# Weight tiles of the projections at multiples of 512 bytes in each partition, in a two-layer hybrid trunk

## The chip, the cores and the metric

The kernel runs on one core of a Trainium2 chip. The metric is the device time of one execution in microseconds; the kernel before is given by the median of three runs. A profiled execution of the same kernel gives the rows that are read here. Engines are named as in the profile: PE is TensorE's matmul, PEld its loading of the stationary operand, DVE is VectorE, ACT ScalarE, POOL GpSimd, SP the engine that issues the weight transfers.

## The reference

Two layers work on 256 tokens of width 2048, in float32. A layer normalises its input, multiplies it by one wide matrix, runs four token mixers of width 512 on the parts (forgetting attention, differential attention, a state-space recurrence in chunks, a diagonal state-space scan), and merges them with gates:

```python
xn = _rmsnorm(h, pre_norm_g[l])
(fq, fk, fv, ff, fg, dq, dk, dv, dg, sz, sxbc, sdt, su, sg, mg) = _combined_projection(xn, w_in[l])
oa = _forgetting_attention(...) * jax.nn.silu(fg)
ob = _differential_attention(...) * jax.nn.silu(dg)
oc = _ssd_branch(sz, sxbc, sdt, ...)
od = _s5_branch(su, ...) * jax.nn.silu(sg)
merged = None
for n, o in enumerate((oa, ob, oc, od)):
    gate = jax.nn.sigmoid(mg[..., n * D_MODEL:(n + 1) * D_MODEL])
    term = gate * (o.astype(h.dtype) @ w_branch[l, n])
    merged = term if merged is None else merged + term
y = merged @ w_out[l]
h = h + _rmsnorm(y, post_norm_g[l])
```

By far the most arithmetic is in the projections: `xn @ w_in`, `o @ w_branch`, the small matrix of the last mixer, and `merged @ w_out`, each with 256 tokens on one side.

## The kernel before, in words

A projection is cut into groups of 512 output columns (one group, `bc`, has 524). `plan()` lists the groups of a layer in the order in which they run. `group()` computes one of them for two blocks of 128 tokens. For each k-tile (128 rows of the weights) it issues three matmuls for token block 0 and three for block 1, all of 512 columns. The factor three comes from the number format: each weight w and each activation x is split into a high and a low part in float32r, and the product is taken as xh·wh + xh·wl + xl·wh (L387, L388, L389). In these matmuls the activation part is the stationary operand and the weight tile is streamed. In the rows `acc<-wh,xh` the streamed tile is named first.

The weights come in chunks of four k-tiles (1 MB) on SP's queue into `raw`, which has three buffers. `prefetch()` then makes two pairs of tiles of each chunk, each for two k-tiles: ScalarE copies `raw` into `wh` (L104), VectorE subtracts to get `wl` (L92). The pools whp and wlp have five buffers each, and take turns. So ten k-tiles go once round the five buffers. Buffers of a pool are all as big as the largest tile in it, 2 x 524 floats, that is 4192 bytes in each partition.

The first chunk, and some chunks around the last projection of each layer, take another way: with `spread=True` the four k-tiles are split one by one into tiles of the pool `blkp` (names bwh and bwl), which has 37 buffers of 2048 bytes in each partition and holds most other activations of a layer too. In the last group of each layer and the first of layer 1 the second token block comes 16 k-tiles behind the first (`lag`). In the program as built, where the framework orders instructions anew by what is ready, the two blocks of layer 1's first group alternate on different k-tiles at the end; in the last group of layer 1 block 0 runs through all k-tiles before block 1. In all other groups the two blocks take each k-tile in turn, so that block 1 reads the weight tile that block 0 has just read.

The stationary tiles (xh, xl, mh, ml from the pool actp; oh, ol, gh, gl from blkp) start at multiples of 512 bytes.

The mixers run between the projections. After each chunk `pump()` takes pieces of them from a queue, up to a budget of VectorE time, and issues them on all engines. Their small matmuls and transposes stand in TensorE's own order between two chunks of a projection. Transposes and several masks use the table `cs`, which is in the first pool, cp, with the residual stream `h` and the parameters.

Pools lie one after the other in each partition in the order in which they are opened: cp, rawp, whp, wlp, actp, blkp, tp. In the kernel as built, `cs` starts at byte 32,896, the first raw buffer at 40,448, the first wh at 65,600, the first wl at 86,560, the first stationary tile of actp at 107,520 and the first blk at 140,288.

Of the kernel before, what the change touches and what calls it, by code (L numbers as in the profile page):

```python
# [10 lines left out]
F32 = mybir.dt.float32  # L11
F32R = mybir.dt.float32r
# [6 lines left out]
L, D, T = 2, 2048, 256  # L19
NBLK = 37  # L20
NW = 5
AHEAD = 1
BUDGET = 1.7
# [3 lines left out]
W = 512  # L27
# [3 lines left out]

# w_in column offsets of the segments
SEG = dict(fq=0, fk=512, fv=1024, ff=1536, fg=1540, dq=2052, dk=2564, dv=3076, dg=3588,
           sz=4100, xs=4612, B=5124, C=5380, dt=5636, su=5644, sg=6156, mg=6668)

# columns of the constant table
C_ID, C_U, C_ST, C_MK, C_COS, C_SIN, C_ONE, NCST = 0, 128, 256, 384, 640, 704, 832, 833
# columns of the per-partition parameter table
P_PRE, P_CW, P_CB, P_ARE, P_AIM, P_LDT, P_D, NPRM = 0, 16, 48, 56, 72, 88, 104, 108
# columns of the row (broadcast) parameter table  # L40
R_B12, R_ALOG, R_SD, R_SUB, NROW = 0, 12, 20, 28, 156


def plan():
    """Order in which one layer consumes its weights: (kind, argument, columns per k-tile, k-tiles)."""
    p = []
    for s in ("fq", "fk", "fv", "bc", "fg", "dq", "dk", "dv", "dg", "xs", "sz", "su", "sg"):
        p.append(("in", s, 524 if s == "bc" else 512, KT))
    for n in range(3):
        for cg in range(4):  # L50
            p.append(("mg", (n, cg), 512, KT))
            p.append(("br", (n, cg), 512, 4))
    for cg in range(4):
        if cg == 3:
            p.append(("glu", 0, 512, 4))
            p.append(("glu", 1, 512, 4))
        p.append(("mg", (3, cg), 512, KT))
    for cg in range(4):
        p.append(("br", (3, cg), 512, 4))
    for cg in range(4):  # L60
        p.append(("out", cg, 512, KT))
    return p
# [3 lines left out]
def trunk(ctx: ExitStack, tc: tile.TileContext, x, xT0, wall, cst, prm, rows, lam, normg, postg, s5b, s5c, out):  # L66
# [3 lines left out]

    cp = ep(tc.tile_pool(name="cp", bufs=1))
    rawp = ep(tc.tile_pool(name="rawp", bufs=3))
    whp = ep(tc.tile_pool(name="whp", bufs=NW))
    wlp = ep(tc.tile_pool(name="wlp", bufs=NW))
    actp = ep(tc.tile_pool(name="actp", bufs=2))
    blkp = ep(tc.tile_pool(name="blkp", bufs=NBLK))
# [12 lines left out]

# [1 line left out]
    def tt(out, a, b, op):  # L91
# [17 lines left out]
    order = [None]  # L109

    def load(out_, in_):
        """on the queue of the weights, in the order of the calls."""
        if order[0] is None:
            order[0] = nc.sync.dma_start(out=out_, in_=in_).ins
        else:
            with tc.issue_after(order[0]):
                order[0] = nc.sync.dma_start(out=out_, in_=in_).ins

# [1 line left out]
    h = [cp.tile([128, D], F32, name=f"h{tb}") for tb in range(2)]  # L120
# [14 lines left out]
    one = cs[:, C_ONE:C_ONE + 1]  # L135

# [1 line left out]
    def rsqrt(dst, ss, n, inv, eps):  # L138
        """dst = 1/sqrt(ss*inv + eps), all [128, n]."""
        v, y, t, p = (small([128, n], f"rq_{c}{n}") for c in "vytp")  # L140
        ts(v, ss, inv, eps, MUL, ADD)
        ts(y.bitcast(I32), v.bitcast(I32), -0.5, 1597463007.0, MUL, ADD)
        for i in range(2):
            if n == 1:
                stt(t, y, v, y, MUL, MUL)
            else:
                tt(t, y, y, MUL)
                tt(t, t, v, MUL)
            ts(p, t, 0.375, -1.25, MUL, ADD)
            tt(t, t, p, MUL)  # L150
            last = V.scalar_tensor_tensor(out=dst if i else y, in0=t, scalar=1.875, in1=y, op0=ADD, op1=MUL)
        return last.ins
# [35 lines left out]

# [1 line left out]
    ex1 = cp.tile([128, L, 26], F32, name="ex1")  # L190
# [6 lines left out]
    def params():  # L197
# [20 lines left out]
        dt = ex1[:, :, 10:26]  # L218
# [3 lines left out]
        yield 1.3  # L222
        # theta and 16*theta, reduced to [-pi, pi], then sin and cos of a quarter, doubled twice
        sh = [128, 2, L, 16]
# [30 lines left out]
        yield 0.5  # L255
        # k = (exp(lam dt) - 1) / lam
        kr, ki_ = S5K[:, 0], S5K[:, 1]
# [20 lines left out]

# [1 line left out]
    def split_T(dst, src, nt, scale=None, gcol=None):  # L280
        """src [128, nt*128] -> dst(i) = (hi, lo), each [128, 128], of the scaled transpose of block i;
        dst(None) = both for all blocks at once."""
        ps = mx()
# [16 lines left out]

# [1 line left out]
    chunks = [ncol for _ in range(L) for _, _, ncol, nk in plan() for _ in range(nk // 4)]  # L302
# [3 lines left out]
    behind = [None]  # L306

    def prefetch(spread=False):
        """loads the next chunk of four k-tiles and splits it into its two float32r parts."""
        ncol = chunks[woff[1]]  # L310
# [14 lines left out]
        for hf in range(2):  # L325
            wh = whp.tile([128, 2, ncol], F32R, tag="wh", name="wh")
            wl = wlp.tile([128, 2, ncol], F32R, tag="wl", name="wl")
            act(wh, raw[:, 2 * hf:2 * hf + 2])
            split_lo(wl, raw[:, 2 * hf:2 * hf + 2], wh)
            loaded.extend((wh[:, kk], wl[:, kk]) for kk in range(2))  # L330
# [8 lines left out]
    queue = []  # L339
# [28 lines left out]
    def group(stat, nk, ncol, evac, budget=BUDGET, lag=0, hook=None):  # L368
        """acc[tb] = stat(tb)^T @ W for one group of columns, token block 1 some k-tiles behind block 0;
        evac(tb, acc) takes each block's."""  # L370
        cuts = [(0, 512)] if ncol == 512 else [(0, ncol // 2), (ncol // 2, ncol // 2)]
# [29 lines left out]

# [1 line left out]
    def pipeline(n, stages, step):  # L403
        """item i's stage j runs in step i + j*step; each stage gives its cost on VectorE."""
        for t in range(n + (len(stages) - 1) * step):
            cost = 0.0
            for j, f in reversed(list(enumerate(stages))):
                if 0 <= t - j * step < n:
                    cost += f(t - j * step)
            yield cost  # L410

    def headpair_T(dst, src, hp, scale=None):
        """dst [128, 2 heads, 256 tokens] from the token-major src[tb]."""
        ps = mx().rearrange("p (h t) -> p h t", h=2)
# [6 lines left out]
    def probs_T(E, nb):  # L421
        """transposes of E [128 q, nb*128] -> [128 k, nb, 128 q] in SBUF."""
        ps = mx()
# [11 lines left out]
    def fox(st):  # L435
# [8 lines left out]
        for kb in range(2):  # L444
# [7 lines left out]
            p3 = ps.rearrange("p (h k) -> p h k", h=4)  # L452
            # lf is -log_sigmoid, so its running sum enters with a plus
            for hd in range(4):
# [141 lines left out]
    def ssd(st):  # L596
# [9 lines left out]
        yield WAIT  # L606
        # decay from each token to the end of chunk 0, and from the start of chunk 1 to each token
        psd = mx()
# [3 lines left out]
        act(dec, psd[:, 0:16], AF.Exp)  # L612
        # the running sums' addends in two exact float32r parts
        Ah, Al = small([128, 2, 8], "Ah", F32R), small([128, 2, 8], "Al", F32R)
# [66 lines left out]
        for tb in range(2):  # L681
# [6 lines left out]
            for g in range(2):  # L688
                L3 = LT[2 * tb + g].rearrange("p (h t) -> p h t", h=4)
                tt(L3, L3, Gm[tb][:, g:g + 1].to_broadcast([128, 4, 128]), MUL)  # L690
                yield 0.6
        # state after chunk 0, and its way into chunk 1
        pst = mx()
# [38 lines left out]
    def s5(st):  # L732
        l = st["l"]
        # tables exp(i theta t), t = 0..15 and 16*(0..15); re/im: which, tile, power
        E1 = [blk("E1", (128, 2, 16, 16)) for _ in range(2)]
# [7 lines left out]
        while n < 16:  # L743
            # power n = (power n/2)^2, then powers n+1 .. 2n-1
            hr, hi = E1[0][:, :, :, n // 2], E1[1][:, :, :, n // 2]
# [19 lines left out]
            n *= 2  # L765
        # C' = C * k
        cr = [blk("s5c", (128, 16, 32)) for _ in range(2)]
# [142 lines left out]

# [1 line left out]
    def new_act(name):  # L912
# [11 lines left out]
    for l in range(L):  # L924
        ss = small([128, 2, 4], "hss")
        st = dict(l=l)
        # transposed input times the gain, not normalised; 1/rms goes in where the products leave PSUM
        if l == 0:
# [98 lines left out]
        for gi, (kind, arg, ncol, nk) in enumerate(plan()):  # L1027
# [70 lines left out]
            else:  # L1098
# [8 lines left out]
                def residual(tb, last):  # L1107
                    """h += y / rms(y) * gain; then the next layer's input, or the output."""
                    s1, r1 = small([128, 1], "ys1"), small([128, 1], "yr1")
# [29 lines left out]

# [1 line left out]
def _layout(i):  # L1141
# [88 lines left out]
```

## Time and profile before

| | |
|---|---|
| median of 3 runs | 1813.01 us (1811.5 to 1814.68) |
| span of the profiled execution | 1811.1 us |
| TensorE busy | 1793.2 us, 8348 matmuls |
| VectorE busy | 1318.5 us |
| ScalarE busy | 862.1 us |
| DMA | 331.32 MB, mean 183 GB/s |

The span runs from the first to the last instruction. In the rows, a matmul is given with the time at which it starts and the time until its result is through, and neighbouring matmuls overlap in that; the pace of TensorE is therefore read from the distances between starts. The granted clock (PEclk) is a share of full speed: 1.00 is the upper of its two levels, 2.4 GHz.

### The profile page before, as it was taken

How to read it: one execution, taken by the hardware profiler on the slowest of the kernel's cores; microseconds unless marked ns; L12 is line 12 of the kernel's file. 1: busy time of each engine (PE TensorE's matmuls, PEld its weight loads, DVE VectorE, ACT ScalarE, POOL GpSimd, SP SyncE). 2: the span in 40 equal slices, each digit the busy share in tenths (PEclk: the TensorE clock that was granted, in tenths of full speed). 3: DMA queues.
4: the chain of work that ended last, by engine and by line, in shares of the span. 5: the costliest groups of instructions: out<-in, count | busy, mean ns of one | idle time of the engine just before them, and what ended most of it. 6: DMA issues, size and time to landing. Idle time of an engine off the chain costs nothing.

```text
span 1811.1 us, 21982 instructions
## 1 busy us (share of the span) xinstructions
PE 1793.2 (99%) x8348; PEld 1460.4 (81%) x8348; DVE 1318.5 (73%) x2358; ACT 862.1 (48%) x1171; POOL 16.5 (1%) x34
## 2 busy tenths in 40 slices
PE   8999999999999999999999999999999999999997
PEld 6888877888878787788879888788888787877886
DVE  6764478887798879765674645689777988787744
ACT  6445445545444444444464454555444444444442
POOL 0000000000000000000000000000000000000000
PEclk9999999999999999999999999999999999999999
DMA  9554543455555545555545445434554554556552
GB/s 344 191 185 149 193 172 134 174 186 197 186 194 180 184 163 210 193 188 179 186 184 188 163 163 186 163 140 172 203 178 162 198 209 175 178 197 208 183 187 94
DMA packets 49434, 331.32 MB, mean 183 GB/s; under 512 B 6064, under 2 KB 6192, under 8 KB 10800
## 3 DMA queue, kind: packets, MB, share of 16 engines
q1 hardware_dynamic: 46928, 322.05, 50.1%
q0 software_dynamic: 2400, 7.87, 1.2%
q8 instruction: 65, 1.06, 0.2%
q14 instruction: 41, 0.34, 0.1%
HBM read 327.80 MB, written 2.10 MB: 182 GB/s over the span
## 4 chain that ended last, share of the span: by engine, by line
PE 97%; DMA 1%; DVE 1%; ACT 0%; issue 0%; SPq 0%; DVEq 0%; ACTq 0%
PE acc L388 30%; PE acc L387 30%; PE acc L389 30%; PE mx L285 1%; DMA raw<-in_wall_dram 1%; PE mx L549 1%; PE mx L433 1%; PE mx L418 1%; PE mx L877 0%; PE mx L846 0%; PE mx L815 0%; PE mx L706 0%; PE mx L425 0%; PE mx L467 0%; DVE wl L92 0%; DVE h L101 0%
## 5 line engine op out<-in xcount | busy, mean ns | idle before, releaser
L92 DVE TENSOR_TENSOR wl<-raw,wh 128x1024 fp32r<-128x1024 f32 (+1 forms) x586 | 714.2, 1223 | 397.6 <-ACT wh L104 396.6
L104 ACT ACTIVATE wh<-raw 128x1024 fp32r<-128x1024 f32 (+1 forms) x586 | 620.4, 1060 | 788.9 <-PE acc L389 731.2
L387 PE MATMUL acc<-wh,xh 128*128 128x512 f32 (+1 forms) x1896 | 737.1, 389 | 0.0
L388 PE MATMUL acc<-wl,xh 128*128 128x512 f32 (+1 forms) x1896 | 735.1, 388 | 0.5 <-DVE wl L92 0.5
L389 PE MATMUL acc<-wh,xl 128*128 128x512 f32 (+1 forms) x1896 | 733.2, 387 | 0.0
L387 PEld LDWEIGHTS acc<-wh,xh 128*128 128x128 f32 x1896 | 356.3, 188 | 78.7 <-issue 3.8
L388 PEld LDWEIGHTS acc<-wl,xh 128*128 128x128 f32 x1896 | 356.4, 188 | 76.9 <-issue 2.0
L389 PEld LDWEIGHTS acc<-wh,xl 128*128 128x128 f32 x1896 | 356.4, 188 | 76.7 <-issue 0.7
L387 PE MATMUL acc<-wh,oh 128*128 128x512 f32 x256 | 101.4, 396 | 0.0
L389 PE MATMUL acc<-wh,ol 128*128 128x512 f32 x256 | 100.8, 394 | 0.0
L388 PE MATMUL acc<-wl,oh 128*128 128x512 f32 x256 | 100.8, 394 | 0.0
L387 PE MATMUL acc<-wh,mh 128*128 128x512 f32 x224 | 88.6, 396 | 0.0
L388 PE MATMUL acc<-wl,mh 128*128 128x512 f32 x224 | 88.4, 394 | 0.0
L389 PE MATMUL acc<-wh,ml 128*128 128x512 f32 x224 | 88.3, 394 | 0.0
L104 ACT ACTIVATE sig<-acc,rhalf 128x512 f32<-128x512 f32 x64 | 44.0, 688 | 32.1 <-PE acc L389 28.6
L389 PEld LDWEIGHTS acc<-wh,ol 128*128 128x128 f32 x256 | 48.1, 188 | 11.1
L388 PEld LDWEIGHTS acc<-wl,oh 128*128 128x128 f32 x256 | 48.1, 188 | 10.7
L387 PEld LDWEIGHTS acc<-wh,oh 128*128 128x128 f32 x256 | 48.1, 188 | 10.6
L389 PEld LDWEIGHTS acc<-wh,ml 128*128 128x128 f32 x224 | 42.1, 188 | 9.7
L387 PEld LDWEIGHTS acc<-wh,mh 128*128 128x128 f32 x224 | 42.1, 188 | 9.6
L388 PEld LDWEIGHTS acc<-wl,mh 128*128 128x128 f32 x224 | 42.1, 188 | 9.5
L864 DVE TENSOR_TENSOR_SCAN s5a<-S5R,s5w 128x256 f32<-128x256 f32 x64 | 40.9, 676 | 0.0
(331 smaller groups left out, 1336.4 us busy)
## 6 DMA issues: line engine op xcount, KB each, us to landing
raw<-in_wall_dram SPq DMA_DIRECT2D x291, 1024.0 KB, 4.8
raw<-in_wall_dram SPq DMA_DIRECT2D x8, 1048.0 KB, 4.9
s5b<-in_s5b_dram POOLq DMA_DIRECT2D x16, 256.0 KB, 3.7
xr<-in_xT_dram SPq DMA_DIRECT2D x8, 256.0 KB, 9.1
h<-in_x_dram SPq DMA_DIRECT2D x2, 1024.0 KB, 8.8
pg<-in_postg_dram POOLq DMA_DIRECT2D x8, 256.0 KB, 4.3
out_dram<-h SPq DMA_DIRECT2D x8, 256.0 KB, 2.8
s5c<-in_s5c_dram POOLq DMA_DIRECT2D x4, 256.0 KB, 4.6
```

Source lines behind the costliest of these rows:

```text
L92: V.tensor_tensor(out=out, in0=a, in1=b, op=op)
L104: A.activation(out, a, f, **kw)
L285: PE.transpose(ps[:, i * 128:(i + 1) * 128], src[:, i * 128:(i + 1) * 128], ident)
L387: PE.matmul(o, lhsT=sh, rhs=rh, start=k == 0, stop=False)
L388: PE.matmul(o, lhsT=sh, rhs=rl, start=False, stop=False)
L389: PE.matmul(o, lhsT=sl, rhs=rh, start=False, stop=k == nk - 1)
L418: PE.transpose(ps[:, i, tb * 128:(tb + 1) * 128], src[tb][:, c:c + 128], ident)
L433: PE.matmul(pso[:, c], lhsT=pt[:, b], rhs=v[b][:, c], start=b == 0, stop=b == nb - 1)
L549: PE.matmul(ps[:, a, 0:nk], lhsT=qT[hd // 2][64 * a:64 * a + 64, hd % 2, qb * 128:(qb + 1) * 128], rhs=kT[hd // 2][64 * a:64 * a + 64, hd ...
L864: V.tensor_tensor_scan(out=a[:, r], data0=rr, data1=w[:, r], initial=0.0, op0=MUL, op1=ADD)
```

## The change

Each tile of wh and wl now begins at a multiple of 512 bytes in its partition. Three edits do it: a tile `pad` of 112 floats (448 bytes) is the first of the pool cp and moves everything behind it; the tiles of the 524-column group are allocated 576 columns wide and used only in their first 524, so that a buffer has 4608 bytes; and a tile `pad2` of 384 floats (1536 bytes) stands in the pool wlp. Nothing is written to the pads or read from them. Instructions, their order and their sizes are otherwise the same. The places of the tiles behind the weights move by 6144 bytes in all. The diff, without comments that it also drops:

```diff
 NBLK = 37
 NW = 5
+KW = 576
+PAD = 112
...
     cp = ep(tc.tile_pool(name="cp", bufs=1))
+
+    pad = cp.tile([128, PAD], F32, name="pad")
     rawp = ep(tc.tile_pool(name="rawp", bufs=3))
     whp = ep(tc.tile_pool(name="whp", bufs=NW))
     wlp = ep(tc.tile_pool(name="wlp", bufs=NW))
+
+    pad2 = wlp.tile([128, 384], F32, tag="pad2", name="pad2", bufs=1)
     actp = ep(tc.tile_pool(name="actp", bufs=2))
...
         for hf in range(2):
-            wh = whp.tile([128, 2, ncol], F32R, tag="wh", name="wh")
-            wl = wlp.tile([128, 2, ncol], F32R, tag="wl", name="wl")
+            kw = ncol if ncol == 512 else KW
+            wh = whp.tile([128, 2, kw], F32R, tag="wh", name="wh")[:, :, 0:ncol]
+            wl = wlp.tile([128, 2, kw], F32R, tag="wl", name="wl")[:, :, 0:ncol]
             act(wh, raw[:, 2 * hf:2 * hf + 2])
```

## Rows read from the trace of the kernel before

**Rows 1.** The page: busy us and share by engine; the chain that ended last.

```profile
PE 1793.2 (99%) x8348; PEld 1460.4 (81%) x8348; DVE 1318.5 (73%) x2358; ACT 862.1 (48%) x1171; POOL 16.5 (1%) x34
...
PE 97%; DMA 1%; DVE 1%; ACT 0%; issue 0%; SPq 0%; DVEq 0%; ACTq 0%
```

**Rows 2.** TensorE's longest wait: us in all, times, longest us.

```profile
PE acc L387 <- ACT bwh L104: 6.9, 2, 6.6
```

**Rows 3.** TensorE's groups by form: count, busy us, mean ns of one.

```profile
L387 PE MATMUL acc<-wh,xh 128*128 128x512 f32 x1768 | 700.6, 396 | 0.0
...
L387 PE MATMUL acc<-wh,oh 128*128 128x512 f32 x256 | 101.4, 396 | 0.0
...
L387 PE MATMUL acc<-wh,mh 128*128 128x512 f32 x224 | 88.6, 396 | 0.0
...
L387 PE MATMUL acc<-wh,xh 128*128 128x262 f32 x128 | 36.4, 285 | 0.0
...
L387 PE MATMUL acc<-wh,gh 128*128 128x512 f32 x32 | 12.8, 399 | 0.0
...
L425 PE MATMUL mx<-cs,E 128*128 128x128 f32 x48 | 10.8, 279 | 0.2 <-ACT pt L104 0.2
...
L285 PE MATMUL mx<-cs,m 128*128 128x128 f32 x64 | 8.3, 272 | 0.0
```

**Rows 4.** Timeline, last projection of layer 1: starts of some k-tiles (block 0).

```profile
1731.51 0.39 PE L387 MATMUL acc<-wh,mh 128*128 128x512 f32 x1
...
1735.67 0.39 PE L387 MATMUL acc<-wh,mh 128*128 128x512 f32 x1
...
1737.05 0.39 PE L387 MATMUL acc<-wh,mh 128*128 128x512 f32 x1
...
1739.83 0.39 PE L387 MATMUL acc<-wh,mh 128*128 128x512 f32 x1
...
1741.24 0.39 PE L387 MATMUL acc<-wh,mh 128*128 128x512 f32 x1
...
1745.41 0.39 PE L387 MATMUL acc<-wh,mh 128*128 128x512 f32 x1
...
1753.73 0.39 PE L387 MATMUL acc<-wh,mh 128*128 128x512 f32 x1
...
1755.14 0.39 PE L387 MATMUL acc<-wh,mh 128*128 128x512 f32 x1
```

**Rows 5.** Timeline, last group of layer 1, tiles from blk, 23 steps.

```profile
1784.31 0.39 PE L387 MATMUL acc<-bwh,mh 128*128 128x512 f32 x1
...
1785.47 0.39 PE L389 MATMUL acc<-bwh,ml 128*128 128x512 f32 x1
...
1789.55 0.39 PE L389 MATMUL acc<-bwh,ml 128*128 128x512 f32 x1
```

**Rows 6.** Timeline, first group of layer 1, tiles from blk, 27 steps.

```profile
923.68 0.39 PE L387 MATMUL acc<-bwh,xh 128*128 128x512 f32 x1
...
929.80 0.39 PE L389 MATMUL acc<-bwh,xl 128*128 128x512 f32 x1
```

**Rows 7.** Stages: us, busy PE, PEld, DVE, ACT, POOL, clock, DMA share, GB/s.

```profile
923.40:930.00 6.60, 6.60 (x30) 5.45 (x30) 5.86 (x15) 4.13 (x7) 0.00 (x0) 1.00 0.95 371
...
500.00:550.00 50.00, 50.00 (x231) 39.99 (x230) 45.61 (x74) 23.38 (x28) 1.08 (x2) 1.00 0.50 179
```

**Rows 8.** Timeline: first and last of 133 cuts in the projections.

```profile
60.54 1.03 PE L418 MATMUL mx<-cs,fq 128*128 128x128 f32 x8
...
1716.73 1.04 PE L285 MATMUL mx<-cs,m 128*128 128x128 f32 x8
```

**Rows 9.** Splits on VectorE: count, ns least/median/most, first and last start.

```profile
L92 DVE TENSOR_TENSOR wl<-raw,wh x586: 1194/1225/1253, 15.2 to 1777.3; 128x1024 fp32r<-128x1024 f32 x191, 128x1048 fp32r<-128x1048 f32 x5
```

**Rows 10.** Timeline, first group of layer 0, last steps of its first chunk.

```profile
14.30 0.39 PE L389 MATMUL acc<-bwh,xl 128*128 128x512 f32 x1
...
14.98 0.39 PE L389 MATMUL acc<-bwh,xl 128*128 128x512 f32 x1
```

## The prediction

> **What bounds the kernel now.** I read the page first. TensorE is busy 1793.2 of the 1811.1 us of the span, and the chain that ended last is TensorE for 97% [rows 1]. The waits say that nothing starves it: its longest kind of wait on another engine adds up to 6.9 us in two places [rows 2]. So weights are ready early, and the time is the number of matmuls times the distance from one start to the next. Busy time hides that distance, because matmuls overlap (each row shows some 395 ns, while a new one starts every 230 ns). I therefore went to the timeline of TensorE and subtracted starts.
>
> Almost all of the work is 512 columns wide and reads a weight tile from the pools of wh and wl: by the groups kept apart by form, L387 has 1768 + 256 + 224 + 32 = 2280 of them, and L388 and L389 as many each, 6840 in all [rows 3]. In the last projection of layer 1 a k-tile is six such matmuls in a row (L387, L388, L389 for token block 0, then for block 1). Ten k-tiles use each of the five buffers of the pool once, with both halves of it. One such round, 60 matmuls, runs from 1731.51 to 1745.41: 13.90 us, or **231.67 ns a matmul**. The reader should see that the k-tiles within it are unequal and that the inequality comes back: the one that starts at 1735.67 takes 1.38 us, the one at 1739.83 takes 1.41 us, and a round later, at 1753.73, the same place in the round takes 1.41 us again [rows 4]. Same shape, same engine state, other buffer: what differs is where in a partition the tile lies. The code gives the places. A buffer of wh or wl holds 2 x 524 floats, 4192 bytes, which is 8 x 512 + 96; so the five buffers start at five different remainders of 512 (64, 160, 256, 352, 448 for wh, 32, 128, 224, 320, 416 for wl, adding up the tiles in front of them).
>
> The trace of before also holds the other case. For the first chunk, and around the last projection of each layer, `prefetch(spread=True)` puts weight tiles into the blk pool (bwh, bwl), whose buffers of 2048 bytes start at multiples of 512 (the first at 140,288 = 274 x 512). They go through the same three lines with the same activations. From 1785.47 to 1789.55 there are 18 steps in 4.08 us: **226.67 ns a matmul** [rows 5]. And with both token blocks interleaved, 27 steps from 923.68 to 929.80 take 6.12 us: again 226.67 [rows 6]. That is not a quiet moment: in the window around the second stretch VectorE is busy 5.86 of 6.60 us, ScalarE 4.13, the DMA engines 95%, and the granted clock is 1.00, as elsewhere [rows 7]. So neither neighbours nor clock explain the 5 ns.
>
> **The change, part by part.** *The weight tiles.* The pad ahead of everything adds 448 bytes, which brings the first wh buffer from 65,600 to 66,048 = 129 x 512; 576 columns instead of 524 make a buffer 4608 bytes = 9 x 512; the second pad (1536 bytes) keeps wl at a multiple of 512 and makes the total shift of the later pools 448 + 10 x 416 + 1536 = 6144 = 12 x 512, so activations and the blk pool keep their remainders. All 6840 matmuls then read from places like those of bwh and bwl. Gain if each goes from 231.67 to 226.67 ns: 6840 x 5.00 ns = **34.2 us**. All of it is on the path, since TensorE is the path.
>
> *What is not gained.* The pace has to settle: when bwh tiles follow wh tiles at 1784.31, the first 5 steps take 1.16 us to 1785.47, where 5 x 226.67 would be 1.133 us, so 0.027 us too much [rows 5]. I charge this once after each interruption. Other matmuls cut the stream of projections 133 times (counted along the timeline, the first and the last in [rows 8]): 133 x 0.027 = 3.6 us. The last step before and the first after a cut have lengths of their own (the first after the cut of [rows 8] lies in the wake of other work), so I take no gain on 2 x 133 steps: 266 x 5 ns = 1.3 us. Net: 34.2 - 3.6 - 1.3 = **29.3 us**.
>
> *The 262-column matmuls* (group bc; 128 on each line at 285 ns [rows 3]) start at multiples of 512 only in part: the second k-tile lies 2304 bytes on, the second cut 1048. No row shows them elsewhere. Bounds: 384 x 5 ns = 1.9 us gained or lost; I take 0, the middle, since half of their starts stay odd.
>
> *The pad before everything* also moves h, the tables cs and the parameters by 448 bytes, to other remainders. Some 460 small matmuls read cs. Those of L285 and L425 read the same table with other operands and take 272 and 279 ns [rows 3]; that 7 ns as the reach of a place gives at most 3.2 us either way. I take 0, because neither row shows which remainder is good for them.
>
> *The splits.* ScalarE's and VectorE's instructions per buffer keep their size. Over all five buffers and three raw buffers, each at another remainder, VectorE's stay within 1194 to 1253 ns, median 1225 [rows 9]; a place costs them nothing that shows. They lie beside TensorE's work on the buffer, 12 x 231 ns = 2.8 us. Cover: the fullest 50 us of VectorE that I found are 45.61 busy [rows 7]; with TensorE 2% faster that becomes 93%, still under the full window. If the cover went there, the loss would be a part of the 1 us that such a window gains, not more. No DMA, wait or instruction is added or moved.
>
> *A rule against the change.* The rows above say that place costs 5 ns. The Trainium skill (TensorE: Matmul & The Clock Gate, Step-by-step: what each phase is for) gives TensorE two independent read ports, one for the streamed operand and one for the stationary; and SBUF — State Buffer, Operand start alignment, asks only for multiples of the element size, adding that this is about legality and not speed. By these alone the sum would be 0, which is the second rival below; the rows disagree, as far as bwh and bwl stand for wh and wl.
>
> **The rivals.**
> 1. *The pace settles anew in each buffer.* The blk tiles lie 2048 bytes apart; the new buffers lie 4608 apart, an odd multiple of 512, so their places alternate in the next higher bit. If that counts as a new place, the 0.027 us fall due at each of 6840 / 12 = 570 buffers: 15.4 us off the gain, 1813.0 - 29.3 + 15.4 = 1799 us. For it: misaligned buffers have a length each [rows 4]. Against: in [rows 6] stationary tiles alternate by 512 bytes and the pace holds.
> 2. *Nothing happens*: bwh and bwl are quick for another reason than place (a tile of one k-tile alone, other neighbours in memory). 1813 us. For it: bwh is another pool with another buffer size; against: the differences among wh's own buffers, which have nothing but place to tell them apart [rows 4].
> 3. *Slower: even places collide in the main loop.* There block 1's L387 reads the same weight tile that block 0's L389 has just read; the long stretches of bwh do not (in [rows 5] one block runs alone, in [rows 6] two different tiles alternate). Now that streamed and stationary operand both start at multiples of 512 each time, the repeat could cost in every k-tile. Price, by the worst buffer of today: 1.41 us a k-tile is 235.0 ns a matmul, 3.3 ns over today's mean, 6840 x 3.3 = 22.6 us: 1836 us. It decides if the repeat costs over 30 ns in each k-tile (6 x 5 ns, what the rest gains). Against: the first chunk of layer 0 lies in blk too and runs in the main loop's order; its step from L389 to L387 at 14.30 is such a repeat, and the 3 steps from there to 14.98 take 0.68 us, 226.67 ns each [rows 10]. That is one repeat, so a small chance stays.
>
> **How the numbers follow.** The profiled span is 1811.1 us and the median of the runs 1813.0, 1.9 more. Span after: 1811.1 - 29.3 = 1781.8; time: 1783.7, say 1784. Chances: forecast 0.76, rival 1 0.10, rival 2 0.09, rival 3 0.05. The range reaches down to no settling cost plus the 262-column gain (1813.0 - 34.2 - 1.9 = 1777) and up to rival 1 (1799), which leaves out rivals 2 and 3, 0.14, and a little. About 0.2% is what a measurement of this kernel can tell from no change. Faster by more: forecast and rival 1, 0.86; within: rival 2, 0.09; slower: rival 3, 0.05.
>
> **What would show it.** In the timeline after, a round of 60 matmuls in the last projection should take 13.60 us instead of 13.90, its ten k-tiles all 1.36 us. The mean duration of the 512-wide groups should fall by some 5 ns from 396, and TensorE's waits stay under 10 us. Rival 1 shows as k-tiles of 1.36 and 1.39 in turn; rival 2 as 1.38 to 1.41 as now; rival 3 as 1.41 throughout, the long step always between L389 of block 0 and L387 of block 1. I am wrong in size, not in kind, if the cuts cost more than 0.027 us each; and wrong in kind if the round is 13.90 us or VectorE turns up among TensorE's waits.

## The result, and the profile after

The changed kernel takes 1783.24 us, the median of four executions, against 1812.68 us of the kernel before: a ratio of 0.9836 (95% interval 0.9822 to 0.9849). Three of the four executions took 1782.19 to 1783.35 us; the fourth took 3613.36 us at a granted clock of 1.00, is left out of the ratio as a slow one, and has no trace that would say why. Forecast were 1784 us, between 1777 and 1799. The profiled span went from 1811.1 to 1781.6 us, 29.5 us less, where the sum had said 29.3.

From the page after, part 1 (busy us by engine), the chain by engine, and the waits of TensorE:

```profile
span 1781.6 us, 21982 instructions
...
PE 1762.9 (99%) x8348; PEld 1458.8 (82%) x8348; DVE 1317.1 (74%) x2358; ACT 861.2 (48%) x1171; POOL 16.4 (1%) x34
...
PE 97%; DMA 1%; DVE 1%; ACT 0%; issue 0%; SPq 0%; DVEq 0%; ACTq 0%
```
```profile
PE acc L394 <- ACT bwh L110: 7.0, 2, 6.5
PE acc L394 <- ACT wh L110: 0.6, 1, 0.6
PE acc L395 <- DVE wl L98: 0.5, 1, 0.5
```

The counts of instructions are those of [rows 1]; only the busy time of PE has moved, by 30.3 us. The weight loads (PEld), VectorE and ScalarE are within 2 us of what they were. TensorE still waits for hardly anything, as in [rows 2]. So the time did not come out of a wait.

The round of ten k-tiles in the last projection of layer 1, as in [rows 4] (L394 is now what L387 was), shows where it came from:

```profile
1733.22 0.39 PE L394 MATMUL acc<-wh,mh 128*128 128x512 f32 x1
...
1734.58 0.39 PE L394 MATMUL acc<-wh,mh 128*128 128x512 f32 x1
...
1735.94 0.39 PE L394 MATMUL acc<-wh,mh 128*128 128x512 f32 x1
...
1744.10 0.39 PE L394 MATMUL acc<-wh,mh 128*128 128x512 f32 x1
...
1745.46 0.39 PE L394 MATMUL acc<-wh,mh 128*128 128x512 f32 x1
...
1746.82 0.39 PE L394 MATMUL acc<-wh,mh 128*128 128x512 f32 x1
```

From 1733.22 to 1746.82 are 13.60 us for 60 matmuls, 226.67 ns each, and every k-tile takes 1.36 us: the long and short places of [rows 4] are gone. Over all 512-wide steps between two such matmuls, the mean distance of starts is 227.2 ns (6762 steps; those of 0.31 us or more, most of them the first after a cut, are left out), against 231.5 before.

### The profile page after: what moved, and what is told of

Same layout as the page of the kernel before. It is cut to its first block, busy times and chain, and to the rows that moved or that the text cites. A ratio compares the mean times of both kernels' runs of the same rounds, so it can differ in the third digit from the quotient of the medians.

```text
span 1781.6 us, 21982 instructions
## 1 busy us (share of the span) xinstructions
PE 1762.9 (99%) x8348; PEld 1458.8 (82%) x8348; DVE 1317.1 (74%) x2358; ACT 861.2 (48%) x1171; POOL 16.4 (1%) x34
## 4 chain that ended last, share of the span: by engine, by line
PE 97%; DMA 1%; DVE 1%; ACT 0%; issue 0%; SPq 0%; DVEq 0%; ACTq 0%
PE acc L394 30%; PE acc L395 30%; PE acc L396 30%; DMA raw<-in_wall_dram 1%; PE mx L291 1%; PE mx L556 1%; PE mx L440 1%; PE mx L425 1%; PE mx L884 0%; PE mx L853 0%; PE mx L822 0%; PE mx L713 0%; PE mx L432 0%; PE mx L474 0%; DVE wl L98 0%; DVE h L107 0%
## 5 line engine op out<-in xcount | busy, mean ns | idle before, releaser
L110 ACT ACTIVATE wh<-raw 128x1024 fp32r<-128x1024 f32 (+1 forms) x586 | 620.6, 1061 | 761.1 <-PE acc L396 697.6
L98 DVE TENSOR_TENSOR wl<-raw,wh 128x1024 fp32r<-128x1024 f32 (+1 forms) x586 | 712.8, 1221 | 372.5 <-ACT wh L110 371.8
L394 PE MATMUL acc<-wh,xh 128*128 128x512 f32 (+1 forms) x1896 | 730.5, 385 | 0.6 <-ACT wh L110 0.6
L395 PE MATMUL acc<-wl,xh 128*128 128x512 f32 (+1 forms) x1896 | 727.1, 383 | 0.5 <-DVE wl L98 0.5
L396 PE MATMUL acc<-wh,xl 128*128 128x512 f32 (+1 forms) x1896 | 725.4, 383 | 0.0
L394 PEld LDWEIGHTS acc<-wh,xh 128*128 128x128 f32 x1896 | 356.1, 188 | 72.3 <-issue 3.8
L395 PEld LDWEIGHTS acc<-wl,xh 128*128 128x128 f32 x1896 | 356.3, 188 | 69.4 <-issue 2.0
L394 PE MATMUL acc<-wh,oh 128*128 128x512 f32 x256 | 100.4, 392 | 0.0
L395 PE MATMUL acc<-wl,oh 128*128 128x512 f32 x256 | 99.7, 389 | 0.0
L394 PE MATMUL acc<-wh,mh 128*128 128x512 f32 x224 | 87.7, 391 | 0.0
L395 PE MATMUL acc<-wl,mh 128*128 128x512 f32 x224 | 87.2, 390 | 0.0
L394 PEld LDWEIGHTS acc<-wh,oh 128*128 128x128 f32 x256 | 48.1, 188 | 9.6
L395 PEld LDWEIGHTS acc<-wl,oh 128*128 128x128 f32 x256 | 48.1, 188 | 9.5
L395 PEld LDWEIGHTS acc<-wl,mh 128*128 128x128 f32 x224 | 42.1, 188 | 8.5
L394 PEld LDWEIGHTS acc<-wh,mh 128*128 128x128 f32 x224 | 42.1, 188 | 8.5
```

The costliest lines, as they stand in the source:

```text
L98: V.tensor_tensor(out=out, in0=a, in1=b, op=op)
L110: A.activation(out, a, f, **kw)
L394: PE.matmul(o, lhsT=sh, rhs=rh, start=k == 0, stop=False)
L395: PE.matmul(o, lhsT=sh, rhs=rl, start=False, stop=False)
L396: PE.matmul(o, lhsT=sl, rhs=rh, start=False, stop=k == nk - 1)
```

## The experiments

Three theories were kept apart. **Theory 1**: what counts is the place of the streamed weight tile relative to the stationary activation tile. **Theory 2**: the absolute place of the streamed tile counts, by the 512-byte stretches it crosses. **Theory 3**: not the place but the size or spacing of buffers counts. And a question beside them: is 512 bytes the period? All twelve kernels are edits of the kernel after; what a diff doesn't show is unchanged. The mean granted clock is 0.998 or 0.999 in the profile of every one of them, as it is before and after, so no difference below is one of the clock. Each time has its ratio to the kernel before with a 95% interval; the round is the one shown above. The rows print times in hundredths of a microsecond; the traces keep starts in nanoseconds, and steps that are given below in whole nanoseconds come from there.

| run | wh and wl, activations (modulo 512) | us | ratio to before | round, us |
|---|---|---|---|---|
| before | five places each, 0 | 1812.7 | 1 | 13.90 |
| after | 0, 0 | 1783.24 | 0.9836 [0.9822, 0.9849] | 13.60 |
| e_par | 0, 0; wl an odd multiple behind wh | 1782.39 | 0.9833 [0.9818, 0.9847] | 13.60 |
| e_w64 | 64, 0 | 1798.99 | 0.9925 [0.9910, 0.9939] | 13.74 |
| e_a64 | 0, 64 | 1824.35 | 1.0064 [1.0047, 1.0081] | 14.00 |
| e_wa64 | 64, 64 | 1783.42 | 0.9839 [0.9824, 0.9854] | 13.60 |
| e_w256 | 256, 0 | 1783.07 | 0.9837 [0.9822, 0.9851] | 13.60 |
| e_w128 | 128, 0 | 1820.04 | 1.0041 [1.0026, 1.0055] | 14.00 |
| e_w32 | 32, 0 | 1823.91 | 1.0062 [1.0047, 1.0077] | 14.00 |
| e_w192 | 192, 0 | 1824.35 | 1.0067 [1.0049, 1.0085] | 14.00 |
| e_w16 | 16 or 272, 0 | 1812.63 | 0.9999 [0.9990, 1.0009] | 13.90 |
| e_wl128 | wh 0, wl 128, 0 | 1816.22 | 1.0020 [1.0011, 1.0030] | 13.87 |
| e_padonly | places of before plus 448, 448 | 1812.82 | 1.0001 [0.9992, 1.0011] | 13.90 |
| e_min | 64 or 320, 64 | 1783.37 | 0.9839 [0.9822, 0.9857] | 13.60 |

**A higher bit of the place (e_par).** The second pad moves behind wl.

```diff
-    pad2 = wlp.tile([128, 384], F32, tag="pad2", name="pad2", bufs=1)
     actp = ep(tc.tile_pool(name="actp", bufs=2))
+    pada = actp.tile([128, 384], F32, tag="pada", name="pada", bufs=1)
```

> Weights and activations stay at multiples of 512; only the second pad moves from ahead of wl to behind it, so that wl lies 23,040 bytes (45 x 512, odd) behind wh instead of 24,576 (48 x 512). Theory of place modulo 512: no change against the changed kernel, 1783 us, k-tiles of 1.36 us. Rival (a higher bit of the place counts too): the pace is lost between L387 and L388 in each k-tile, at up to 5 ns a matmul 1800 to 1813 us.

1782.39 us, the round 13.60: whether wl lies an odd or an even multiple of 512 behind wh makes no difference. The second pad could as well stand behind wl.

**Relative or absolute (e_w64, e_a64, e_wa64).** Weights alone, activations alone, and both are moved by 64 bytes.

```diff
 # e_w64
+    padw = whp.tile([128, 16], F32, tag="padw", name="padw", bufs=1)
     wlp = ep(tc.tile_pool(name="wlp", bufs=NW))
-    pad2 = wlp.tile([128, 384], F32, tag="pad2", name="pad2", bufs=1)
     actp = ep(tc.tile_pool(name="actp", bufs=2))
+    pada = actp.tile([128, 368], F32, tag="pada", name="pada", bufs=1)
 # e_a64: no padw, pada of 400 floats
 # e_wa64: padw of 16 floats, pada of 384
```

> All wh and wl buffers begin 64 bytes past a multiple of 512, the activations at multiples of 512 as in the changed kernel. Theory 1 (what counts is the place of the streamed tile relative to the stationary one): slow again, between 228.8 and 235 ns a matmul, 1796 to 1836 us, near 1810. Theory 2 (the absolute place of the streamed tile counts, by the 512-byte stretches it crosses): slow too. Theory 3 (not the place but the equal or larger buffers): 1783 us.

> wh and wl at multiples of 512, all activations (xh, xl, mh, ml, oh, ol, and the blk pool with bwh and bwl) 64 bytes past one. Theory 1 (relative place): slow for wh and wl, 1796 to 1836 us, while bwh and bwl, which moved along with the activations, keep 226.67 ns. Theory 2 (absolute place of the streamed tile): 1783 us, and bwh and bwl lose their pace. Theory 3: 1783 us, bwh at 226.67 ns.

> Weights and activations both 64 bytes past a multiple of 512, so that their relative place is that of the changed kernel. Theory 1 (relative place): 1783 us, 226.67 ns. Theory 2 (absolute place): as slow as with the weights alone moved, 1796 to 1836 us.

The weights alone cost 15.8 us over the changed kernel, the activations alone 41.1, both together 0.2. That is theory 1, on all three; theory 2 had the second and third the other way round, and theory 3 had no change at all. Nor is it the place of the tiles relative to `raw`, from which ScalarE and VectorE make them: the raw buffers lie in the same places in the three runs, so that distance is the changed kernel's in e_a64, which is slow, and 64 bytes off it in e_wa64, which is quick. Within the one run e_a64 the timeline has both sides: the weight tiles of wh, now 64 bytes behind their stationary tiles, and those of blk, which moved along with them.

```profile
1773.79 0.39 PE L394 MATMUL acc<-wh,mh 128*128 128x512 f32 x1
1774.03 0.39 PE L395 MATMUL acc<-wl,mh 128*128 128x512 f32 x1
1774.26 0.39 PE L396 MATMUL acc<-wh,ml 128*128 128x512 f32 x1
...
1787.79 0.39 PE L394 MATMUL acc<-wh,mh 128*128 128x512 f32 x1
...
1797.35 0.39 PE L396 MATMUL acc<-bwh,ml 128*128 128x512 f32 x1
...
1800.07 0.39 PE L396 MATMUL acc<-bwh,ml 128*128 128x512 f32 x1
```

The wh round takes 14.00 us, 233.3 ns a matmul, in steps of 233, 233 and 234 ns; the 12 steps of bwh from 1797.35 to 1800.07 take 2.72 us, 226.67 ns. The tiles of wh start at multiples of 512 and are slow; those of bwh start 64 bytes past one, as their stationary tiles do, and are quick.

**How fine, and which period (e_w256, e_w128, e_w32, e_w192, e_w16).** The diff is that of e_w64 with 64, 32, 8 and 48 floats in `padw`, and with `pada` making up the rest of 384. For 16 bytes the tiles are cut out of the buffers of the changed kernel four columns further on:

```diff
-            kw = ncol if ncol == 512 else KW
-            wh = whp.tile([128, 2, kw], F32R, tag="wh", name="wh")[:, :, 0:ncol]
-            wl = wlp.tile([128, 2, kw], F32R, tag="wl", name="wl")[:, :, 0:ncol]
+            wh = whp.tile([128, 2, KW], F32R, tag="wh", name="wh")[:, :, 4:4 + ncol]
+            wl = wlp.tile([128, 2, KW], F32R, tag="wl", name="wl")[:, :, 4:4 + ncol]
```

> wh and wl 256 bytes past a multiple of 512, activations at multiples of 512. If 256 is multiple enough (a smaller period of the place), 1783 us and 226.67 ns. If the period is 512, the pace is lost: 1796 to 1825 us, as at 64 bytes ahead (1799) or behind (1824).

> wh and wl 128 bytes past a multiple of 512. Period 128 or less: 1783 us. Otherwise slow, 1796 to 1825 us. If the cost grew with the distance from the multiple, more than at 64 bytes ahead (1799).

> wh and wl 32 bytes past a multiple of 512. If the cost grows with the distance: between 1783 and 1799, near 1791 us. If any distance costs about as much as 64 bytes do: 1796 to 1825 us.

> wh and wl 192 bytes past a multiple of 512, activations at one. Relative to 256 that is 64 behind, as with the activations moved 64 ahead. If the period is 256, the same steps as there, 231 and 236 ns in turn, and 1824 us. If not, something else than 1824, up to 1836 us.

> Buffers as in the changed kernel, but the tiles use columns 4 to 515 of them, so that each streamed tile begins 16 bytes past a multiple of 256 (ScalarE and VectorE write two runs of 2048 bytes instead of one of 4096). If any place off the multiple of 256 costs, 1796 to 1825 us as with 32 bytes (1824). If 32 bytes is the finest step that counts, 1783 us.

256 bytes are as good as 0 (1783.07 us), and 192 bytes give the time of 64 behind (1824.35 us both, the round 14.00), so the period that counts for the time is 256 bytes, not 512. The expectation had the single steps of the two alike, too, and they are not: e_w192 goes 235 or 236 and 231 ns in turn, as expected, but e_a64 goes 233, 233 and 234 ns. Between two multiples, no place that was tried comes near the time of a multiple: 16 bytes cost 29 us, 32 bytes 41, 64 bytes 16, 128 bytes 37. The cost does not grow with the distance, which the middle value expected of e_w32 (1791) had supposed. One round each, from multiples of 256 and off them:

```profile
1732.97 0.39 PE L395 MATMUL acc<-wh,mh 128*128 128x512 f32 x1
...
1746.57 0.39 PE L395 MATMUL acc<-wh,mh 128*128 128x512 f32 x1
```
```profile
1768.55 0.40 PE L395 MATMUL acc<-wh,mh 128*128 128x512 f32 x1
...
1782.55 0.40 PE L395 MATMUL acc<-wh,mh 128*128 128x512 f32 x1
```

The first is e_w256, 13.60 us, the second e_w128, 14.00. In e_w16 ScalarE and VectorE write two runs instead of one; their mean times per buffer are 1060 and 1221 ns, against 1061 and 1220 in the changed kernel, and TensorE's longest kind of wait stays at 7.0 us in all, so the 29 us are TensorE's pace there too.

**One weight tile of two out of place (e_wl128).**

```diff
-    pad2 = wlp.tile([128, 384], F32, tag="pad2", name="pad2", bufs=1)
+    padl = wlp.tile([128, 32], F32, tag="padl", name="padl", bufs=1)
     actp = ep(tc.tile_pool(name="actp", bufs=2))
+    pada = actp.tile([128, 352], F32, tag="pada", name="pada", bufs=1)
```

> wl alone 128 bytes past a multiple of 512, wh at one. With both moved by 128 the time was 1820 us, 37 us over the changed kernel. If each stream that is out of place pays by itself, a third of the matmuls (L388's) pays: 1783 + 37 / 3 = 1795 us, and in the timeline one step in three is longer than 227 ns. If the pace as a whole is lost as soon as one of three is out of place: 1810 to 1824 us.

1816.22 us: 33 us over the changed kernel for a third of the matmuls, where both tiles out of place cost 37. That each stream pays for itself is refuted. The timeline shows how it is lost:

```profile
1765.44 0.40 PE L395 MATMUL acc<-wh,mh 128*128 128x512 f32 x1
1765.67 0.39 PE L396 MATMUL acc<-wl,mh 128*128 128x512 f32 x1
1765.90 0.40 PE L397 MATMUL acc<-wh,ml 128*128 128x512 f32 x1
1766.14 0.39 PE L395 MATMUL acc<-wh,mh 128*128 128x512 f32 x1
1766.37 0.39 PE L396 MATMUL acc<-wl,mh 128*128 128x512 f32 x1
1766.59 0.39 PE L397 MATMUL acc<-wh,ml 128*128 128x512 f32 x1
1766.83 0.40 PE L395 MATMUL acc<-wh,mh 128*128 128x512 f32 x1
...
1779.31 0.40 PE L395 MATMUL acc<-wh,mh 128*128 128x512 f32 x1
```

The step that follows the well-placed L397 at 1765.90 is 0.24 us too, as long as any; the whole round takes 13.87. In nanoseconds this k-tile's six steps are 232, 232, 234, 229, 228 and 231, where the changed kernel has 226 or 227 for each. One misplaced stream sets its neighbours back as well, so all three have to be in place.

**Parts of the change (e_padonly, e_min).** The pad ahead of everything alone, with buffers of 4192 bytes; and wider buffers alone, 544 columns, with no pad.

```diff
 # e_padonly
-    pad2 = wlp.tile([128, 384], F32, tag="pad2", name="pad2", bufs=1)
...
-            kw = ncol if ncol == 512 else KW
+            kw = ncol
 # e_min
-KW = 576
+KW = 544
...
-    pad = cp.tile([128, PAD], F32, name="pad")
...
-    pad2 = wlp.tile([128, 384], F32, tag="pad2", name="pad2", bufs=1)
```

> One part of the change alone: the 448 bytes ahead of everything; buffers of 4192 bytes and no second pad, so weights, activations and blk move together and every streamed tile keeps the place relative to its stationary tile that it has in the kernel before. Relative place: 1812.5 us, a round of 13.90 us with the k-tiles of before one by one. If absolute places, or those of cs and h, count: a few us away from it, and other k-tiles are the long ones. Bound from the prediction for cs and h: 3.2 us either way.

> No pads; only the buffers of wh and wl become 544 columns wide, 4352 bytes = 17 x 256. Weights, activations and blk then all lie at 64 past a multiple of 256 (64 or 320 past one of 512). If a place relative to the stationary tile of a multiple of 256 is all that is needed, 1783 us, a round of 13.60 us, with 4544 bytes less in each partition than the change takes. If 512 is needed somewhere, k-tiles of 1.36 and of more alternate: 1790 to 1803 us.

The pad alone moves every tile and changes no relative place: 1812.82 us, a ratio of 1.0001 to before, and of the round in its timeline these k-tiles:

```profile
1767.48 0.39 PE L393 MATMUL acc<-wh,mh 128*128 128x512 f32 x1
...
1768.89 0.39 PE L393 MATMUL acc<-wh,mh 128*128 128x512 f32 x1
...
1777.23 0.39 PE L393 MATMUL acc<-wh,mh 128*128 128x512 f32 x1
...
1778.60 0.39 PE L393 MATMUL acc<-wh,mh 128*128 128x512 f32 x1
```

These are the places in the round of the two k-tiles that the prediction read in [rows 4], and they take 1.41 and 1.37 us again, although all absolute places are others. (The second one's 1.38 us in the prediction is a difference of rounded starts; the trace of before has 1.373 us for it, and this one has 1.373 too.) In nanoseconds all ten k-tiles of the round, from 1767.48 here and from 1739.83 before, agree within 1: 1409, 1386, 1398, 1387, 1386, 1387, 1390, 1373, 1391 and 1393 here, against 1410, 1385, 1399, 1386, 1387, 1387, 1390, 1373, 1391 and 1392. The run also answers the question of cs and h, which moved here as they do in the change: the effect is nothing that can be measured. The wider buffers alone reach 1783.37 us:

```profile
1732.19 0.39 PE L392 MATMUL acc<-wh,mh 128*128 128x512 f32 x1
...
1745.79 0.39 PE L392 MATMUL acc<-wh,mh 128*128 128x512 f32 x1
```

13.60 us with no tile at a multiple of 512, and 4544 bytes less in each partition than the change takes. No run was faster than the changed kernel by more than their intervals; e_min is the cheaper way to the same time.

## Why the prediction was right

*The bound.* TensorE's pace was the time: its busy time fell by 30.3 us, the span by 29.5, with all else in place.

*The gain per matmul.* 231.67 to 226.67 ns in the round was forecast and is what the round shows, 13.90 to 13.60. The stretches of bwh were a true sample of what a well-placed tile does: the tiles of wh, in other pools and with buffers of another size, took on the same 226.67 ns with their place, and lost it again in e_w64 and e_a64. Over the whole kernel the means of 231.5 and 227.2 ns, over 6762 steps, differ by some 29 us, which is nearly all of the 29.5.

*The cost of cuts.* I charged 0.027 us for each of 133. The mean, 227.18 ns, lies 0.51 ns over 226.67; times 6762 steps that is 3.5 us, against 3.6 charged. It also lies where the prediction put it: by the trace's nanoseconds, some 3.2 us of it fall on the first twelve steps after a cut, and from the thirty-first on the mean is 226.7 ns. After one cut of the kernel after, by eight transposes, the rows read:

```profile
1688.81 1.04 PE L291 MATMUL mx<-cs,m 128*128 128x128 f32 x8
1689.60 0.48 PE L394 MATMUL acc<-wh,mh 128*128 128x512 f32 x1
1689.92 0.40 PE L395 MATMUL acc<-wl,mh 128*128 128x512 f32 x1
...
1693.78 0.39 PE L394 MATMUL acc<-wh,mh 128*128 128x512 f32 x1
```

The first step after the cut is 0.32 us, a length of its own, as the prediction set aside; the 17 from 1689.92 take 3.86 us where 17 x 226.67 is 3.853. This cut costs less than 0.027 us; some others cost more. And the passage from wh to bwh tiles that [rows 5] had cost 0.027 us costs nothing now: the five steps that begin at 1754.98 take 1.13 us. What was read there was therefore not the price of an interruption as such. That the cuts cost as much on the mean, 3.5 us / 133 = 0.026 us, is luck in the price, though not in the kind of the term.

```profile
1754.98 0.39 PE L394 MATMUL acc<-bwh,mh 128*128 128x512 f32 x1
...
1756.11 0.39 PE L396 MATMUL acc<-bwh,ml 128*128 128x512 f32 x1
```

*What was taken as 0.* The 262-column groups went from 285 to 283 ns on L387's line and little on the others, under 1 us in all. The small matmuls that read cs keep their 279 and 272 ns, and e_padonly puts the pad's effect within its interval. The splits: the prediction took the cover from a window that is not the fullest. VectorE was busy 49.22 of 50 us from 666.89 on already before, and is busy 49.20 of 50 from 1539.20 on after, so there was hardly any cover left to lose and the 93% of the prediction is not the fullest stretch. The term still came out at 0, because TensorE's wait for VectorE stays at 0.5 us. The rows are the groups by form and, in the second fence (before, then after), the stage's us, then busy PE, PEld, DVE, ACT and POOL, clock, DMA share and GB/s.

```profile
L394 PE MATMUL acc<-wh,xh 128*128 128x262 f32 x128 | 36.2, 283 | 0.0
...
L432 PE MATMUL mx<-cs,E 128*128 128x128 f32 x48 | 10.8, 279 | 0.2 <-ACT pt L110 0.2
...
L291 PE MATMUL mx<-cs,m 128*128 128x128 f32 x64 | 8.3, 272 | 0.0
```
```profile
666.89:716.89 50.00, 50.00 (x235) 40.19 (x234) 49.22 (x85) 22.36 (x27) 0.00 (x0) 1.00 0.50 174
...
1539.20:1589.20 50.00, 50.00 (x239) 40.89 (x238) 49.20 (x84) 22.98 (x27) 0.00 (x0) 1.00 0.49 175
```

*A small miss.* The mean duration of the 512-wide groups was to fall by some 5 ns from 396; L387's group with xh fell to 393 and the one with mh to 391, 3 to 5 ns. The duration of a matmul overlaps its neighbours and is the poorer measure; the distance of starts is the better.

*The rivals.* Rival 1 (the pace settles anew in each buffer) fell in the change itself and in e_par and e_min, where neighbouring buffers lie an odd multiple of 512 apart, in e_min an odd multiple of 256. Rival 2 (bwh quick for another reason than place) fell with the change, which gave the tiles of wh that pace, and with e_w64, where the same buffers lose it 64 bytes further on. It could not fall by bwh itself: no run moves bwh and bwl against their stationary tiles, and they keep a median step of 226 to 227 ns in all of them. Rival 3 (the repeat of a tile in the main loop) did not come; its price, 1836 us, was also too high for what a bad place does: the worst of the places tried gives 1824.

*What was right for too narrow a reason.* The prediction spoke of multiples of 512 bytes, as the change does. The runs show that neither 512 nor the absolute place is needed: of the places tried, the quick ones are those where the distance from streamed to stationary tile is a multiple of 256. That the stationary tiles lay at multiples of 512 before and after made the two rules give the same forecast. The prediction kept them there with the second pad, without saying why their place should count; e_a64, where every tile of wh and wl lies at a multiple of 512 and the time is 1824 us, shows that the gain hung on it. Moving both operands by 64 bytes and moving the activations alone differ by 41 us, so the place of one operand counts only against that of the other. The Trainium skill (TensorE: Matmul & The Clock Gate, Step-by-step: what each phase is for) gives TensorE two independent read ports for the two operands. That does not lead one to expect such a dependence; here the measurement decides.

*What stays open* is which of the two reads gives way. The loading of stationary tiles takes as long as before (median 188 ns in the kernel before, in the one after and in e_w64, 187 to 188 in e_a64), so the delay is not in the duration that the profile gives to a load. In the timeline the load for the next matmul (L395) starts within a hundredth of a microsecond of the present matmul (L394), here in the kernel after:

```profile
1733.22 0.39 PE L394 MATMUL acc<-wh,mh 128*128 128x512 f32 x1
...
1733.22 0.19 PEld L395 LDWEIGHTS acc<-wl,mh 128*128 128x128 f32 x1
```

That it meets the stream in the same part of the memory is the likely reading, but it is only argued: no run here takes one of the two reads away. The runs do not tell either whether the stationary tile that counts is the one in use or the one being loaded, since all stationary tiles of a run lie at the same remainder, nor why 64 bytes cost 16 us one way and 41 the other.

## What to carry to other kernels

Where TensorE is the bound and float32r tiles of 512 columns are streamed against 128-column stationary tiles, look at the distances between starts in the timeline, buffer by buffer: if equal matmuls have unequal distances that return with the round of the pool, the places of the tiles are the first thing to test. Equal distances do not clear the places: in e_a64 every k-tile takes 1.40 us. Give the pools of both operands buffers whose size is a multiple of 256 bytes and let the pools start at the same remainder of 256, so that the distance of any two tiles is a multiple of it (in e_w64 the buffers have such a size, but the pools start 64 bytes apart). One odd-sized tile in a pool (524 columns here) shifts all its buffers. A tile of the same kind that happens to lie well elsewhere in the same trace gave the right forecast here, 226.67 ns.

## What was not expected of the hardware

- Only the relative place counts, with a period of 256 bytes: 1783.4 us with both operands at 64, 1799.0 and 1824.4 us with one of them moved.
- The cost off the multiple has no simple order in the distance: 16 bytes 1812.6 us, 32 bytes 1823.9, 64 bytes 1799.0, 128 bytes 1820.0, 192 bytes 1824.4. Three different distances (32, 128, and 192, which is 64 behind) end at the same round of 14.00 us, 233.3 ns a matmul, though their times over the whole kernel differ by up to 4 us.
- One misplaced stream of three (wl at 128) costs nearly all that wh and wl out of place cost: 1816.2 against 1820.0 us. The kernel before, whose buffers lie at five different places, did better at 1812.7 us than most kernels whose buffers all lie at one wrong place.
